# Hybrid attention and recurrence layer: K's norm buffers, the K/V weight splits and the recurrence's sums of squares put elsewhere

## The chip, the cores and the metric

The kernel runs on one core of a Trainium2 chip. The metric is the device time of one execution in microseconds (us); before and after are compared as medians of several runs. A trace of one execution, taken by the hardware profiler, is the other source: its times count from the start of its span. The engines are TensorE (PE: matrix products; its weight loads are PEld), VectorE (DVE), ScalarE (ACT), GpSimd (POOL) and SyncE (SP, which only starts transfers). Each works through its own instructions in a fixed order and waits on semaphores.

## The reference

One layer over 512 tokens with 2048 features, in float32. Cut to what matters:

```python
h = rms_norm(x, norm_w)
proj = einsum('bsd,de->bse', h, w_in)
q, k, v, g_attn, xr, g_lru = split(proj, SPLITS)
# attention: 8 query heads, 2 key/value heads of 128
q, k = rms_norm per head, then axial rotation
attn_out = softmax(q k^T / sqrt(128)) v
# recurrence: 8 blocks of 128 features, two directions
xc = conv_4_taps(xr) + conv_b
r = sigmoid(xc wa + ba);  i = sigmoid(xc wx + bx)
log_a = -8 * r * softplus(-lam);  a = exp(log_a)
h_t = a_t * h_(t-1) + sqrt(-expm1(2 log_a)) * (i * xc)     # forward and backward, summed
mixed = concat(rms_norm(attn_out) * silu(g_attn), rms_norm(lru_out) * silu(g_lru))
out = x + einsum('bse,ed->bsd', mixed, w_out)
```

## The kernel before, in words

**Products.** Every float32 matrix is split into a high half (a cast by ScalarE, line 228 for weights) and a low half (a subtraction by VectorE, line 229). A product of two such matrices is three products on TensorE: high-high, high-low and low-high (`mm3`, lines 153 to 155).

**Projections.** The weights of a projection come in chunks of 256 rows by 512 columns: `wload` starts a transfer of one chunk into a ring of three slots (`wring`, transfer on line 215) and splits it in two tiles (`wsplit`). The split tiles go into four buffers each for high and low in the pool `xw`; once the pool `wx` has been opened (inside `kv`), every second tile goes there, and there are eight. A projection of 512 columns takes eight chunks. For K/V and Q it is `proj_tok`, which calls `tok_block`: for each chunk c and each of four token tiles t it issues six products (one "unit", two row tiles of three products) into the PSUM bank of t, and yields. So a bank is complete in the last of the eight chunks, and the four banks of tag `pj` are evicted by ScalarE with a scale (`evac_tok`, line 629) before the next projection may write them.

**Stages and weaving.** The products of TensorE stand in the order in which they are written. `weave(fill, chain)` advances the projection by as many units as the chain of other work yields. In order: the recurrence's inputs (two halves of 512 columns), K and V together, Q's first half, Q's second half, the gates woven with attention, and the output. The recurrence's blocks are computed in pairs: the first four blocks (half 0) beside the second input projection, the last four (half 1) beside the K/V projection, and K's and V's own work (`kv`) beside Q's.

**Order on the other engines.** ScalarE, VectorE and, in these stages, SP and GpSimd are ordered when the program is built: a greedy scheduler gives each engine, whenever it is free by the scheduler's own timing, the ready instruction of highest priority. Priority is the place in the program; `tc.high_priority(n)` moves a block's place n instructions forward (AHEAD is 600 for weights, 300 for the recurrence's convolution; without n it goes to the front). `tc.issue_after(ins)`, and `behind(those)` for several, put the instructions of a block behind `ins` in the queue of its own engine. The order is then fixed, and on the chip each engine keeps to it.

**The recurrence** (`lru_pair`, two blocks at a time): split of the gates' weights and convolution (lines 532 to 548); after `steps[b]` units, twelve products per block and four sigmoids (line 559); the gating multiply i * xc (line 563); after `rest` units, tanh (569), exp (575) and sqrt (579) on ScalarE, then on VectorE the multiplies 582 and 583, two scans (586) and the sum of both directions (591). Its tiles lie in the pool `lru`, which is closed after the last pair. The pools `rot`, `qkv` and `wx`, opened later, get their places in memory that `lru` had, and their tiles wait for the release of the tiles that lay there.

**K and V** (`kv`, beside Q): K's norm and rotation (`norm_rope`: squares of each head with a sum on line 641, an inverse root by GpSimd on 374 and 375, multiplies on 646 to 655) in buffers of `rot`; at unit 20 the split of V (695, 696); then the recurrence's sums of squares (`lru_squares`, lines 596 to 603: four squares by ScalarE, the last three in one buffer `hsq`, each added by VectorE, and a last add by GpSimd); then K is turned (291), written to DRAM (299) and read back (321); at units 46 and 50 its two heads are split (685); then the sums are halved (854 to 857), and at unit 54 a product with ones (863) spreads them over all partitions. Its result is turned into an inverse root (864, 868), and the recurrence's outputs are multiplied with it (873). Q's first half passes through the same `norm_rope` and is turned and sent aside at unit 32, its second half after unit 64. Attention's first heads are split on line 685 as well.

**Sums of output weights.** Beside all this, SP copies rows of `w_out` in DRAM (936, behind the last weight transfer in SP's queue) and GpSimd starts adding transfers (939), from Q's first half on behind its own last inverse root.

Of the kernel before, what the change touches and what calls it, by code (L numbers as in the profile page):

```python
# [63 lines left out]
def hybrid_kernel(  # L64
# [373 lines left out]
    def tok_block(acc, w, r0, c0, lh, ll, nk):  # L438

        acc += [pj() for _ in range(NT)]  # L440
        for c in range(nk // 2):
            ws = wload(w, r0 + c * 2 * P, c0)
            for t in range(NT):
                ts_ = slice(t * P, (t + 1) * P)
                for k, (wh, wl) in enumerate(ws):
                    kk = 2 * c + k
                    mm3(acc[t], lh[kk][:, ts_], ll[kk][:, ts_], wh, wl, kk == 0, kk == nk - 1)
                yield c, t

    def proj_tok(c0, acc):  # L450
        yield from tok_block(acc, w_in, 0, c0, xh, xl, KT)
# [55 lines left out]
    def lru_half(half, acc, done=()):  # L507
# [13 lines left out]
        for b in range(0, 4, 2):  # L521
            bs = slice(b, b + 2)
            steps = ((6, 4, 8, 4), (10, 7, 9, 6))[half][bs]
            yield from lru_pair(4 * half + b, xrs[bs], grs[bs], steps, 99 if half and b else 0, mm if half else pj)

    def lru_pair(n0, xrs, grs, steps, rest, bank):

        xcs, cs, rs, is_, ths = [], [], [], [], []
        for n, xr, gr in zip((n0, n0 + 1), xrs, grs):
            with tc.high_priority(AHEAD // 2):  # L530
# [18 lines left out]
                cs.append((gh, gl, ch, cl))  # L549
        for b, n in enumerate((n0, n0 + 1)):  # L550
# [11 lines left out]
            i = is_[b]  # L562
            nc.vector.tensor_mul(i, i, xcs[b][:, None, :].broadcast_to([P, 2, SEQ]))
        yield rest
        for b, n in enumerate((n0, n0 + 1)):
            ths.append(b4())
            for d in range(2):
                j = d * NB + n
                nc.scalar.activation(
                    ths[b][:, d, :], rs[b][:, d, :], AF.Tanh, scale=c2[:, j : j + 1]  # L570
                )
# [21 lines left out]
    def lru_squares():  # L593

        hsum = pools["rot"].tile([P, 2, SEQ], F32, tag="hsum", name="hsum")
        nc.scalar.activation(hsum, hp[0], AF.Square)
        for pair in hp[1:]:
            yield 2
            sq = pools["rot"].tile([P, 2, SEQ], F32, tag="hsq", bufs=1, name=nm("hsq"))
            nc.scalar.activation(sq, pair, AF.Square)  # L600
# [32 lines left out]
    def norm_rope(es, nh, tab):  # L633
# [3 lines left out]
        for e in es:  # L637
            r = pools["rot"].tile([P, nh], F32, tag=f"rr{nh}", bufs=NT, name=nm("rr"))
            for h in range(nh):
                sq = pools["rot"].tile([P, HD], F32, tag="sh", bufs=1, name=nm("sh"))  # L640
# [3 lines left out]
        for t, (e, r) in enumerate(zip(es, rs)):  # L644
            sq = pools["rot"].tile([P, nh, HD], F32, tag="sq", bufs=2, name=nm("sq"))
# [41 lines left out]
    def kv(es):  # L687
        turned_k = sent(norm_rope(es, NKV, rk), NKV)
# [8 lines left out]
        yield from lru_squares()  # L697
# [4 lines left out]
        for h in range(NKV):  # L702
# [3 lines left out]
            those = split_head(pair, h, kth[h], ktl[h])  # L706
        parts = halved(
# [613 lines left out]
    def kv_proj():  # L1321
        yield from proj_tok(C_K, a3)
# [10 lines left out]
    def q_proj(c0, acc):  # L1333
        yield from proj_tok(c0, acc)
        rot[:] = norm_rope(evac_tok(acc, ev), G, rq)
# [181 lines left out]
```

## Time and profile before

| what | value |
|---|---|
| median of 3 runs | 627.7 us (627.63 to 629.04) |
| the profiled execution | 627.59 us |
| its span, first to last instruction | 625.8 us |
| TensorE busy in the span | 618.3 us |
| VectorE | 495.0 us |
| ScalarE | 359.7 us |
| GpSimd | 104.4 us |

Stages in the profiled execution, read off TensorE's order: K/V from about 106 to 161 us with four groups of gate products of half 1 among them, Q's first half from about 161, its second half from about 207, the gates and attention from about 251, the output stage from about 469.

How rows are read. In a row in order of time: start (us), time it took (us; of all of them together where xN stands at the end), engine, line, operation, what it writes `<-` what it reads, shapes; in brackets the idle time of the engine just before it and what ended that. In a group by line the two numbers behind the first bar are the busy time in us and the mean of one in ns, behind the second bar the idle time ahead. In the list of waits: who, for whom, us in total, times, the longest. A PE row lasts longer than the distance between two starts, because products overlap in the pipeline; the pace is the distance.

### The profile page before, as it was taken

Reading aid. Unit: us, or ns where it says so; the run is one execution under the profiler, and the core shown is the slowest. Engines: PE = TensorE matmul, PEld = TensorE weight load, DVE = VectorE, ACT = ScalarE, POOL = GpSimd, SP = SyncE. Lnnn points to the kernel's source line nnn. Section 1 sums busy time; section 2 is a strip of 40 time slices with the busy share of each in tenths; the row PEclk is TensorE's granted clock in tenths of the full one; section 3 lists DMA queues with packets and bytes.
Section 4 is the critical chain, followed back from the end, with each engine's and each line's share of the span. In section 5 each row is a group of like instructions: output and inputs, shape, how many; then the busy total and the mean of one; then the engine's idle time right before and its main releaser. Section 6 shows DMA issues by size and latency. Waiting matters only on the chain.

```text
span 625.8 us, 8286 instructions
## 1 busy us (share of the span) xinstructions
PE 618.3 (99%) x2740; PEld 510.2 (82%) x2740; DVE 495.0 (79%) x785; ACT 359.7 (57%) x646; POOL 104.4 (17%) x142
## 2 busy tenths in 40 slices
PE   9999999999999899999999999999999999999997
PEld 7888888887888688888888888888888888888886
DVE  6874878997798886887887887549979866886885
ACT  4596689959945833645485547338346633443441
POOL 3001111112003532622123222100210101011000
PEclk9999999999999999999999999999999999999999
DMA  8999958678674499579569646932995677797342
GB/s 292 309 330 276 209 140 207 149 186 197 181 229 152 152 209 248 128 199 272 171 197 261 201 136 185 261 92 77 282 251 190 211 254 246 264 362 217 135 135 101
DMA packets 75498, 129.71 MB, mean 207 GB/s; under 512 B 6872, under 2 KB 30528, under 8 KB 75456
## 3 DMA queue, kind: packets, MB, share of 16 engines
q1 hardware_dynamic: 67344, 111.70, 57.2%
q0 software_dynamic: 7936, 17.36, 14.7%
q8 instruction: 21, 0.34, 0.2%
q14 instruction: 21, 0.17, 0.1%
q10 hardware_dynamic: 176, 0.14, 0.1%
HBM read 111.34 MB, written 38.80 MB: 240 GB/s over the span
## 4 chain that ended last, share of the span: by engine, by line
PE 88%; ACT 5%; DVE 4%; issue 1%; DMA 1%; POOL 0%; ACTq 0%
PE pj L153 15%; PE pj L154 15%; PE pj L155 15%; PE mm L1067 14%; PE pj L1067 11%; PE mm L155 5%; PE mm L154 5%; PE mm L153 5%; PE pj L418 2%; ACT wh L228 1%; DVE wl L229 1%; DMA wr<-in_w_in_dram 1%; DVE b L586 1%; PE mm L263 1%; ACT b L559 1%
## 5 line engine op out<-in xcount | busy, mean ns | idle before, releaser
L228 ACT CAST wh<-wr 128x512 fp32r<-128x512 f32 x142 | 84.7, 618 | 85.9 <-PE pj L154 32.3
L154 PE MATMUL pj<-x,wh 128*128 128x512 f32 x304 | 118.3, 389 | 0.0
L155 PE MATMUL pj<-x,wl 128*128 128x512 f32 x304 | 118.3, 389 | 0.0
L153 PE MATMUL pj<-x,wh 128*128 128x512 f32 x304 | 118.3, 389 | 0.0
L229 DVE TENSOR_TENSOR wl<-wr,wh 128x512 fp32r<-128x512 f32 x144 | 98.9, 712 | 20.4 <-ACT wh L228 18.4
L915 ACT CAST wh<-wr 128x1024 fp32r<-128x1024 f32 (+1 forms) x72 | 60.6, 860 | 76.1 <-PE mm L1067 37.5
L916 DVE TENSOR_TENSOR wl<-wr,wh 128x1024 fp32r<-128x1024 f32 (+1 forms) x72 | 68.6, 983 | 30.1 <-ACT wh L915 30.0
L153 PE MATMUL pj<-wh,x 128*128 128x512 f32 x192 | 74.9, 390 | 2.3 <-ACT ev L629 2.3
L154 PE MATMUL pj<-wl,x 128*128 128x512 f32 x192 | 74.9, 390 | 0.2 <-DVE wl L229 0.2
L155 PE MATMUL pj<-wh,x 128*128 128x512 f32 x192 | 74.7, 389 | 0.0
L154 PEld LDWEIGHTS pj<-x,wh 128*128 128x128 f32 x304 | 57.1, 188 | 11.9
L153 PEld LDWEIGHTS pj<-x,wh 128*128 128x128 f32 x304 | 57.1, 188 | 11.9
L155 PEld LDWEIGHTS pj<-x,wl 128*128 128x128 f32 x304 | 57.1, 188 | 11.8
L939 POOL DMA_DIRECT2D t<-in_w_out_dram x40 | 33.3, 896 | 134.5 <-DMA t<-in_w_out_dram 77.6
L1067 PE MATMUL mm<-wh,ml 128*128 128x512 f32 x126 | 49.0, 389 | 0.0
L1067 PE MATMUL mm<-wh,mh 128*128 128x512 f32 x126 | 49.0, 389 | 0.0
L1067 PE MATMUL mm<-wl,mh 128*128 128x512 f32 x126 | 49.0, 389 | 0.0
L153 PEld LDWEIGHTS pj<-wh,x 128*128 128x128 f32 x192 | 36.0, 188 | 10.3 <-ACT ev L629 2.9
L154 PEld LDWEIGHTS pj<-wl,x 128*128 128x128 f32 x192 | 36.0, 188 | 8.0 <-DVE wl L229 0.6
L155 PEld LDWEIGHTS pj<-wh,x 128*128 128x128 f32 x192 | 36.0, 188 | 7.5
L739 POOL TENSOR_SCALAR p<-p,sm 128x512 f32<-128x512 f32 x32 | 23.6, 742 | 89.7 <-DVE sm L738 89.7
L1067 PE MATMUL pj<-wl,mh 128*128 128x512 f32 (+1 forms) x100 | 38.5, 385 | 0.0
(229 smaller groups left out, 1167.7 us busy)
## 6 DMA issues: line engine op xcount, KB each, us to landing
wr<-in_w_in_dram SPq DMA_DIRECT2D x71, 512.0 KB, 5.1
wr<-in_w_out_dram SPq DMA_DIRECT2D x21, 512.0 KB, 5.2
t<-in_w_out_dram POOLq DMA_DIRECT2D x40, 256.0 KB, 7.5
wr<-t SPq DMA_DIRECT2D x40, 256.0 KB, 5.3
pd<-u SPq DMA_DIRECT2D x16, 512.0 KB, 3.5
pt<-pd SPq DMA_DIRECT2D x64, 128.0 KB, 4.0
t<-in_w_out_dram SPq DMA_DIRECT2D x24, 256.0 KB, 5.2
wr<-in_w_out_dram SPq DMA_DIRECT2D x22, 256.0 KB, 4.9
```

Source lines behind the costliest of these rows:

```text
L153: nc.tensor.matmul(acc, lh, rh, start=start, stop=False)
L154: nc.tensor.matmul(acc, lh, rl, start=False, stop=False)
L155: nc.tensor.matmul(acc, ll, rh, start=False, stop=stop)
L228: copy(hi, raw[:, k, :]).ins,
L229: nc.vector.tensor_sub(lo, raw[:, k, :], f(hi)).ins,
L263: nc.tensor.transpose(pt[:, t * P : (t + 1) * P], xc[:, t, ks], ident)
L418: nc.tensor.matmul(acc[e], w[:, e * P : (e + 1) * P], x_[2 * c + k], start=c == k == j == 0, stop=False,)
L739: last_pool[0] = nc.gpsimd.tensor_scalar(p, p, sm, 0.0, op0=ALU.mult, op1=ALU.add).ins
L915: nc.scalar.copy(hi[:, to], b)
L916: nc.vector.tensor_sub(lo[:, to], b, f(hi[:, to]))
L939: nc.gpsimd.dma_start(dst, src, accum_op=ALU.add)
L1067: nc.tensor.matmul(dst[s][:, es], lh[:, ts_], rh[:, es], start=i == ends_[0] and j == 0, stop=i == ends_[1] and j == 2,)
```

## The change

- `tok_block` gets `early`: with 1, a chunk's transfer and split are written one chunk ahead of its products. The K/V projection uses it.
- In half 1, the first pair's `rest` is 4 units instead of 0, and the second pair's first step 5 instead of 9, so that the gate products keep their places. In that pair the tanh instructions are queued behind the last weight cast written by then (chunk 6 of K/V), and the gating multiplies move behind the tanh in the program and behind that chunk's splits in their queue.
- `norm_rope` is told its pool. K's buffers go to `rope`, which is open since the start, under tags of their own; Q's stay in `rot`.
- `lru_squares` moves from V's split to four units behind K's second head, with its squares behind that head's cast in ScalarE's queue (its other member, VectorE's subtraction, binds nothing here, as only the squares stand in that block). The steps of `kv` are then: V at unit 20, K turned and sent at 22, read back at 28, heads at 40 and 44, squares from 48, halving at 54, the product with ones at 58.

```diff
@@ -435,11 +435,14 @@
                     mm3(acc[e], wh[:, es], wl[:, es], xh[kk], xl[kk], kk == 0, kk == KT - 1)
                 yield c, e
 
-    def tok_block(acc, w, r0, c0, lh, ll, nk):
+    def tok_block(acc, w, r0, c0, lh, ll, nk, early=0):
 
         acc += [pj() for _ in range(NT)]
+        ahead = []
         for c in range(nk // 2):
-            ws = wload(w, r0 + c * 2 * P, c0)
+            for n in range(c + len(ahead), min(c + 1 + early, nk // 2)):
+                ahead.append(wload(w, r0 + n * 2 * P, c0))
+            ws = ahead.pop(0)
             for t in range(NT):
                 ts_ = slice(t * P, (t + 1) * P)
                 for k, (wh, wl) in enumerate(ws):
@@ -447,8 +450,8 @@
                     mm3(acc[t], lh[kk][:, ts_], ll[kk][:, ts_], wh, wl, kk == 0, kk == nk - 1)
                 yield c, t
 
-    def proj_tok(c0, acc):
-        yield from tok_block(acc, w_in, 0, c0, xh, xl, KT)
+    def proj_tok(c0, acc, early=0):
+        yield from tok_block(acc, w_in, 0, c0, xh, xl, KT, early)
 
     def weave(fill, chain):
 
@@ -520,8 +523,8 @@
             xrs = [*done, *evac_bc(acc[len(done) :])]
         for b in range(0, 4, 2):
             bs = slice(b, b + 2)
-            steps = ((6, 4, 8, 4), (10, 7, 9, 6))[half][bs]
-            yield from lru_pair(4 * half + b, xrs[bs], grs[bs], steps, 99 if half and b else 0, mm if half else pj)
+            steps = ((6, 4, 8, 4), (10, 7, 5, 6))[half][bs]
+            yield from lru_pair(4 * half + b, xrs[bs], grs[bs], steps, (4, 99)[b // 2] if half else 0, mm if half else pj)
 
     def lru_pair(n0, xrs, grs, steps, rest, bank):
 
@@ -547,6 +550,12 @@
                 nc.scalar.copy(ch, xc)
                 nc.vector.tensor_sub(cl, xc, f(ch))
                 cs.append((gh, gl, ch, cl))
+
+        def gated(b):
+            nc.vector.tensor_mul(
+                is_[b], is_[b], xcs[b][:, None, :].broadcast_to([P, 2, SEQ])
+            )
+
         for b, n in enumerate((n0, n0 + 1)):
             yield steps[b]
             gh, gl, ch, cl = cs[b]
@@ -559,16 +568,21 @@
                     nc.scalar.activation(
                         dst[:, d, :], pg, AF.Sigmoid, bias=v1(bias + d * NB + n)
                     )
-            i = is_[b]
-            nc.vector.tensor_mul(i, i, xcs[b][:, None, :].broadcast_to([P, 2, SEQ]))
+            if not 0 < rest < 99:
+                gated(b)
         yield rest
         for b, n in enumerate((n0, n0 + 1)):
             ths.append(b4())
             for d in range(2):
                 j = d * NB + n
-                nc.scalar.activation(
-                    ths[b][:, d, :], rs[b][:, d, :], AF.Tanh, scale=c2[:, j : j + 1]
-                )
+                with behind(split_done[-1][:1] if 0 < rest < 99 else ()):
+                    nc.scalar.activation(
+                        ths[b][:, d, :], rs[b][:, d, :], AF.Tanh, scale=c2[:, j : j + 1]
+                    )
+        if 0 < rest < 99:
+            for b in range(2):
+                with behind(split_done[-1]):
+                    gated(b)
         for b, n in enumerate((n0, n0 + 1)):
             for d in range(2):
                 j, r = d * NB + n, rs[b][:, d, :]
@@ -590,14 +604,16 @@
                 hp[n // 2] = hring.tile([P, 2, SEQ], F32, name=nm("hs"))
             nc.vector.tensor_add(hp[n // 2][:, b, :], i[:, 0, :], i[:, 1, :])
 
-    def lru_squares():
+    def lru_squares(those):
 
         hsum = pools["rot"].tile([P, 2, SEQ], F32, tag="hsum", name="hsum")
-        nc.scalar.activation(hsum, hp[0], AF.Square)
+        with behind(those):
+            nc.scalar.activation(hsum, hp[0], AF.Square)
         for pair in hp[1:]:
             yield 2
             sq = pools["rot"].tile([P, 2, SEQ], F32, tag="hsq", bufs=1, name=nm("hsq"))
-            nc.scalar.activation(sq, pair, AF.Square)
+            with behind(those):
+                nc.scalar.activation(sq, pair, AF.Square)
             nc.vector.tensor_add(hsum, hsum, sq)
         sums["l"] = hsum[:, 0, :]
         nc.gpsimd.tensor_add(sums["l"], sums["l"], hsum[:, 1, :])
@@ -630,19 +646,19 @@
                 res.append(e)
         return res
 
-    def norm_rope(es, nh, tab):
+    def norm_rope(es, nh, tab, home, n=""):
 
         es = [e[:, : nh * HD].rearrange("p (h d) -> p h d", d=HD) for e in es]
         rs = []
         for e in es:
-            r = pools["rot"].tile([P, nh], F32, tag=f"rr{nh}", bufs=NT, name=nm("rr"))
+            r = pools[home].tile([P, nh], F32, tag=f"rr{n}", bufs=NT, name=nm("rr"))
             for h in range(nh):
-                sq = pools["rot"].tile([P, HD], F32, tag="sh", bufs=1, name=nm("sh"))
+                sq = pools[home].tile([P, HD], F32, tag=f"sh{n}", bufs=1, name=nm("sh"))
                 nc.scalar.activation(sq, e[:, h, :], AF.Square, accum_out=r[:, h : h + 1])
             rsqrt_mean(r, r, HD, nh)
             rs.append(r)
         for t, (e, r) in enumerate(zip(es, rs)):
-            sq = pools["rot"].tile([P, nh, HD], F32, tag="sq", bufs=2, name=nm("sq"))
+            sq = pools[home].tile([P, nh, HD], F32, tag=f"sq{n}", bufs=2, name=nm("sq"))
             nc.vector.tensor_mul(e, e, r[:, :, None].broadcast_to([P, nh, HD]))
             for s in range(2):
                 nc.vector.tensor_mul(
@@ -685,7 +701,7 @@
         return nc.scalar.copy(hi, src).ins, nc.vector.tensor_sub(lo, src, f(hi)).ins
 
     def kv(es):
-        turned_k = sent(norm_rope(es, NKV, rk), NKV)
+        turned_k = sent(norm_rope(es, NKV, rk, "rope", "k"), NKV)
         yield 20
         opened("wx", "right")
         for t in range(NT):
@@ -694,7 +710,6 @@
             vh[t], vl[t] = vt[:, 0, :], vt[:, 1, :]
             nc.scalar.copy(vh[t], vv)
             nc.vector.tensor_sub(vl[t], vv, f(vh[t]))
-        yield from lru_squares()
         yield 2
         drain(turned_k)
         yield 6
@@ -704,6 +719,8 @@
             kt = pools["qkv"].tile([P, 2, SEQ], F32R, tag="kt", bufs=NKV, name=nm("kt"))
             kth[h], ktl[h] = kt[:, 0, :], kt[:, 1, :]
             those = split_head(pair, h, kth[h], ktl[h])
+        yield 4
+        yield from lru_squares(those)
         parts = halved(
             sums["l"],
             lambda: pools["rope"].tile([P, SEQ], F32R, tag="kv", bufs=NT, name=nm("kv")),
@@ -1319,7 +1336,7 @@
     kvs = []
 
     def kv_proj():
-        yield from proj_tok(C_K, a3)
+        yield from proj_tok(C_K, a3, 1)
         kvs.extend(
             evac_tok(
                 a3, lambda: pools["rope"].tile([P, SEQ], F32, tag="kv", bufs=NT, name=nm("kv"))
@@ -1332,7 +1349,7 @@
     opened("qkv", "right")
     def q_proj(c0, acc):
         yield from proj_tok(c0, acc)
-        rot[:] = norm_rope(evac_tok(acc, ev), G, rq)
+        rot[:] = norm_rope(evac_tok(acc, ev), G, rq, "rot")
 
     def both():
         yield from q_proj(C_Q, a4)
```

## The prediction

> **What bounds the kernel now.** I read the page's busy shares first, then PE's waits, then PE, ScalarE and VectorE in order of time around each wait.
>
> ```profile
> PE 618.3 (99%) x2740; PEld 510.2 (82%) x2740; DVE 495.0 (79%) x785; ACT 359.7 (57%) x646; POOL 104.4 (17%) x142
> PE pj L153 <- ACT ev L629: 2.3, 1, 2.3
> PE pj L154 <- DVE wl L229: 0.2, 1, 0.2
> PEld mm L155 <- DVE q L685: 0.3, 1, 0.3
> 204.49 0.39 PE L155 MATMUL pj<-wh,x 128*128 128x512 f32 x1
> 207.13 0.50 PE L153 MATMUL pj<-wh,x 128*128 128x512 f32 x1 [2.26 <-ACT ev L629]
> 207.47 0.40 PE L154 MATMUL pj<-wl,x 128*128 128x512 f32 x1
> 214.00 0.39 PE L155 MATMUL pj<-wh,x 128*128 128x512 f32 x1
> 144.43 0.39 PE L153 MATMUL pj<-wh,x 128*128 128x512 f32 x1
> 144.98 0.50 PE L154 MATMUL pj<-wl,x 128*128 128x512 f32 x1 [0.16 <-DVE wl L229]
> 145.32 0.39 PE L155 MATMUL pj<-wh,x 128*128 128x512 f32 x1
> 188.39 0.39 PE L153 MATMUL pj<-wh,x 128*128 128x512 f32 x1
> 189.30 0.39 PE L154 MATMUL pj<-wl,x 128*128 128x512 f32 x1
> ```
>
> TensorE is busy 99% of the span, so only its gaps can be won. In a stretch without gaps four products start 189.30 - 188.39 = 0.91 us apart: 0.227 us each, 1.36 us a unit of six, 5.44 us a chunk of 24. Against that pace the two gaps ahead of the places that the change touches cost:
>
> - K/V chunk 6: from 144.43 to 145.32 two steps take 0.89 us where 0.45 would do: **0.44 us**. The low half of the weights came late.
> - Q's second half: from 204.49 to 207.47 two steps take 2.98 us: **2.53 us** lost. The next 28 steps, to 214.00, take 6.53 us for 6.35: **0.18 us** more.
>
> All that can be won is 0.44 + 2.53 + 0.18 = 3.15 us, 0.5% of 627.59 us. A measurement of this kernel can tell about 0.3%, which is 1.9 us, so the large gap alone decides between faster and the same.
>
> Why the large gap is there:
>
> ```profile
> 202.54 1.06 ACT L600 ACTIVATE hsq<-hs 128x1024 f32<-128x1024 f32 x1 [4.34 <-DVE hsum L601]
> 204.93 1.06 ACT L600 ACTIVATE hsq<-hs 128x1024 f32<-128x1024 f32 x1 [0.81 <-DVE hsum L601]
> 206.40 0.68 ACT L629 ACTIVATE ev<-pj,rstd 128x512 f32<-128x512 f32 x1
> 201.23 1.22 DVE L601 TENSOR_TENSOR hsum<-hsum,hsq 128x1024 f32<-128x1024 f32 x1
> 186.29 3.09 DVE L229 TENSOR_TENSOR wl<-wr,wh 128x512 fp32r<-128x512 f32 x5
> ```
>
> The second half of Q needs the PSUM banks of the first. The first half's last chunk starts 5.44 us ahead of the second half's due time, 204.49 + 0.23 = 204.72, so at 199.28, and the first bank gets its last product one unit later, near 200.6. Its eviction (L629) runs at 206.40, nearly 6 us later. ScalarE stood 4.34 us in front of a sum of squares, which has one buffer and waits for VectorE's add of the one before, and VectorE reached that add (201.23) only between K's rotations. The evictions were queued behind it.
>
> **The change, part by part.** No operation is added or removed on any engine; buffers and the order change.
>
> *Squares behind K's heads.* Four squares, three adds, GpSimd's add and the halving leave the stretch before 206. The first bank can then be evicted near 201.3 (200.6 plus 0.68) and is wanted at 204.7. Each later bank is ready and wanted one unit after the one before, so the spare time of some 3.4 us holds for all four. Are the second half's weights next in line? Q chunk 5 starts three chunks ahead of 204.72, at 188.39, and at 189.38 VectorE had split five tiles from there on, two and a half chunks: they are not. Gain 2.53 + 0.18 us.
>
> What the move costs: the all-ones product (L863) that spreads the sums stands in TensorE's written order, and goes from unit 54 to unit 58 of Q.
>
> ```profile
> 237.34 0.40 PE L863 MATMUL mm<-kv,ones_r 128*128 128x512 f32 x1
> 207.39 1.60 POOL L603 TENSOR_TENSOR hsum<-hsum 128x512 f32<-128x512 f32 x1 [8.81 <-DVE hsum L601]
> 227.86 1.24 DVE L685 TENSOR_TENSOR kt<-lq,kt 128x512 fp32r<-128x512 f32 x2
> 229.12 0.69 DVE L857 TENSOR_TENSOR kv<-hsum,kv 64x512 fp32r<-64x512 f32 x1
> 225.43 0.81 POOL L939 DMA_DIRECT2D t<-in_w_out_dram  x1 [3.77 <-issue]
> ```
>
> It comes at 237.34 + 5.44 - 3.15 = 239.63. Its operand was ready at 229.81 (the end of L857), with 7.5 us to spare. Now the chain starts late. At worst nothing of it runs before K's heads are through VectorE, at 229.10 - 3.15 = 225.95 (Q's rotation holds VectorE until then). From there: three adds (3.7) with two squares between them (2.1), GpSimd's 1.60, and the three steps of the halving at 0.69 (2.1; the first two put at the row of the third): 9.5 us. With 0.2 us at each of seven hand-overs (an estimate; from the add's end at 202.45 to the square at 202.54 it was 0.09) and four weight splits of 0.62 let in ahead: 13.4 us, ready at 239.4. GpSimd's add (L603) also moves past the DMA adds that GpSimd issues from 219 on; where one of them stands before it, as the one that waited 3.77 us to issue, the end is 243.2. At the other end the adds have slipped into VectorE's gaps before Q's rotation, and only GpSimd's step and the halving follow: 4.5 us, ready at 230.4. Needed is 239.63. I take zero: the DMA adds leave GpSimd free most of the time, and VectorE's gaps take the first adds. For the range: 0 to 3.6 us.
>
> The spread being later, its followers are later too:
>
> ```profile
> 246.54 1.22 DVE L873 TENSOR_TENSOR hs<-hs,gbc 128x1024 f32<-128x1024 f32 x1
> 251.67 0.69 DVE L646 TENSOR_TENSOR ev<-ev,rr 128x512 f32<-128x512 f32 x1 [3.91 <-POOL rr L375]
> 265.86 1.28 DVE L685 TENSOR_TENSOR q<-lq,q 128x512 fp32r<-128x512 f32 x2
> ```
>
> From the product at 237.34 to the last of the four normalizing multiplies at 247.76 VectorE's train takes 10.4 us, then idles 3.91 us. From 239.63 it would end at 250.05, while the rotation of Q's second half wants VectorE at 251.67 - 3.15 = 248.52. That overlap is 1.5 us. The rotation leads to the split of attention's first query (265.86), for which TensorE already waits a little (the 0.3 us row). So 0 to 1.5 us comes back there. The rotation goes first by its place in the program, so it waits for less than one multiply: I take **0.5 us**.
>
> *K's buffers with the rotation tables.* K's squares no longer wait for memory that the recurrence holds, as they did until 187.77:
>
> ```profile
> 185.69 2.19 ACT L228 CAST wh<-wr 128x512 fp32r<-128x512 f32 x4 [2.59 <-DVE b L586]
> 187.77 0.31 ACT L641 ACTIVATE sh<-kv 128x128 f32<-128x128 f32 x1
> 182.47 0.62 ACT L228 CAST wh<-wr 128x512 fp32r<-128x512 f32 x1 [4.13 <-PE pj L155]
> 219.29 1.14 ACT L685 CAST kt<-lq 128x512 fp32r<-128x512 f32 x2 [2.02 <-DMA lq<-qd]
> ```
>
> ScalarE waits of 4.13 and 2.59 us stand before 182.47 and 185.69; the eight squares, 0.31 us each with a short readout behind, fit in there. VectorE's part follows the recurrence's scans, so K is turned and sent aside several us earlier, and its heads land before 219. On SP the write and four reads back pass in front of weight loads; those run chunks ahead of TensorE, so they hide it. Worth nothing by itself: no wait of TensorE is for K.
>
> The danger is the other way. A K multiply let in between two dependent steps of the recurrence delays the last scan (L586), on which the cast at 185.69 waits for its memory. That cast belongs to Q chunk 5, whose low halves are the first two of the five at 186.29, done near 187.5; TensorE wants the second at 189.30, or 188.86 once it is 0.44 us ahead. About 1.3 us to spare, against one multiply of some 0.4 us: zero, up to 0.3 us if ScalarE's part of the recurrence also slips by two casts.
>
> *Weights ahead of the tangents.*
>
> ```profile
> 140.25 1.95 ACT L569 ACTIVATE b<-b,c 128x512 f32<-128x512 f32 x3
> 142.09 1.14 ACT L228 CAST wh<-wr 128x512 fp32r<-128x512 f32 x2
> 143.12 1.21 DVE L563 TENSOR_TENSOR b<-b,k 128x1024 f32<-128x1024 f32 x1
> 144.25 1.28 DVE L229 TENSOR_TENSOR wl<-wr,wh 128x512 fp32r<-128x512 f32 x2
> 154.58 2.35 DVE L583 TENSOR_TENSOR b<-b,b 128x1024 f32<-128x1024 f32 x2
> ```
>
> Chunk 6's casts (142.09) stand behind three tangents, and its low halves (144.25) behind a gating multiply. The casts' buffers come free with chunk 4's last products, 5.44 us before 144.43, at 139. Put first, the casts end near 141.5 and the low halves near 142.5, two us in time: the 0.44 us goes. The last tangent still ends when it did, since the same instructions fill the same time; the gating multiplies come some 2.5 us later, and are first read at 154.58. The second pair's convolution is written four units (5.44 us) later, but VectorE takes it by readiness, long before its own products. The earlier loads change nothing, as a load waits for its ring slot; the copies of the output weights that SP holds behind the last load come up to a chunk later and are first read in the output stage.
>
> **Sum.** 0.44 + 2.53 + 0.18 - 0.5 = 2.65 us. The profiled execution took 627.59 us (span 625.8), 0.11 below the median of the runs: 624.94 against it, so **625.0 us** for the median.
>
> **Rivals.**
>
> *Eaten* (0.13): ScalarE and VectorE take K's work in front of the recurrence's in several places, and the last scan is 3 us late. Then chunk 5 waits 3 - 1.3 = 1.7 us: 626.7 us. For it: the recurrence and K meet on both engines, and both orders are the scheduler's. Against: the recurrence's steps stand earlier in the program.
>
> *Not what it says* (0.06): another blocked instruction stands before the evictions, K's head cast waiting for its transfer, as it did 2.02 us at 219.29. K is now ready earlier, so this wait comes nearer to 201 to 205. It must exceed the 3.4 us to spare. If it restores the gap, only 0.44 us is left: 627.1 us.
>
> *Spread late by one wait* (0.08): the chain's worst end, behind one DMA add: TensorE waits 243.2 - 239.63 = 3.6 us at L863, 628.6 us.
>
> *Slower* (0.14): the squares chain stands behind waits of both engines. With one DMA add before GpSimd's step (3.77) and one square on ScalarE behind a cast that waits for TensorE (the 4.13 us row), the operand comes at 239.4 + 7.9 = 247.3; TensorE waits 7.7 us at L863: 632.7 us. It is slower by over 0.3% from a wait of 2.65 + 1.9 = 4.5 us, an operand after 244.1. For it: the chain has little to spare at its worst end, and before, both kinds of wait fell into this stretch. Against: it needs VectorE to have no gap for the adds from 205 on, too.
>
> *GpSimd in the recurrence's way* (0.03): K's inverse roots would run beside the last scans.
>
> ```profile
> L375 POOL TENSOR_TENSOR rr<-rr,nhalf 128x2 f32<-128x2 f32 x4 | 3.2, 810 | 0.3
> L374 POOL TENSOR_SCALAR rr<-rr 128x2 f32<-128x2 f32 x4 | 1.8, 456 | 44.9 <-ACT sh L641 44.9
> 190.89 0.75 POOL L375 TENSOR_TENSOR rr<-rr,nhalf 128x2 f32<-128x2 f32 x1
> 190.68 0.42 DVE L696 TENSOR_TENSOR v<-kv,v 128x256 fp32r<-128x256 f32 x1
> 191.75 0.42 DVE L654 TENSOR_TENSOR kv<-kv,rk 128x256 f32<-128x256 f32 x1
> ```
>
> If each held VectorE for its whole time, the last scan would be 3.2 + 1.8 = 5.0 us late and chunk 5 would wait 3.7 us: 628.7 us, within 0.3%. Against: a two-input VectorE operation that ran into GpSimd's power at 190.89 took 0.42 us, as the one without it at 191.75. [...]
>
> **How the numbers follow.** My forecast has 0.56. It reaches from 624.4 (nothing given back), less some scatter, to 625.8 (the 0.3% bound). Eaten, not what it says, the spread late by one wait and GpSimd's hold lie within 0.3%: 0.13 + 0.06 + 0.08 + 0.03 = 0.30. Slower: 0.14. The range runs from 624.0, since runs of one kernel scatter (627.63 to 629.04 before), to 628.6, which takes in all that lies within 0.3% but GpSimd's hold, and leaves out the slower one.
>
> **What would show it.** Right: no wait of TensorE for L629 and none for L229 near 144; the eviction at 201 to 203 with no L600 before it; L641 on K before 182; L600 and L601 after K's L685; L863 without a gap near 239.6, its operand's last step (L857) before that. Wrong: a gap at L863, one at Q's chunk 5 near 188, or over 1 us at attention's first product near 263.

## The result, and the profile after

| | before | after |
|---|---|---|
| median of 4 runs each, on one chip | 628.37 us (627.63 to 629.39) | 638.43 us (636.71 to 638.56) |
| ratio, 95% interval | | 1.0153 [1.0128, 1.0178] |
| the profiled execution; its span | 627.59 us; 625.8 us | 638.56 us; 636.8 us |

The kernel after is slower by 1.5%, where 625.0 us was forecast. Its line numbers are shifted; the first column below is the line of the kernel before.

| before | after | what it is |
|---|---|---|
| L559, L569 | L568, L579 | sigmoid, tanh of the recurrence |
| L601, L603 | L617, L619 | VectorE's add of squares, GpSimd's last add |
| L629, L641 | L645, L657 | eviction, square of a head |
| L685 | L701 | split of a head |
| L854, L857, L863 | L871, L874, L880 | first and last step of the halving, spread product |
| L939 | L956 | adding transfer that GpSimd starts |

First the page's line of busy times and all waits of TensorE that the view of waits lists (us in total, times, longest).

```profile
PE 622.7 (98%) x2740; PEld 512.7 (81%) x2740; DVE 494.7 (78%) x785; ACT 359.9 (57%) x646; POOL 107.2 (17%) x142
PE mm L880 <- DVE kv L874: 6.6, 1, 6.6
PE pj L154 <- DVE wl L229: 1.4, 1, 1.4
PE mm L155 <- DVE q L701: 0.9, 1, 0.9
PE mm L1213 <- PEq L1519: 0.8, 1, 0.8
PE mm L153 <- ACT b L568: 0.4, 2, 0.2
```

The eviction's wait of before (2.3 us) is gone, as forecast: the first bank is evicted when TensorE is through with it.

```profile
203.78 0.69 ACT L645 ACTIVATE ev<-pj,rstd 128x512 f32<-128x512 f32 x1 [0.74 <-PE pj L155]
```

In the wait's place stand the spread product's, one at Q chunk 5, one at attention's first query, and two short ones of the last gate products for the sigmoids. VectorE and ScalarE are as busy as before. Now the largest, TensorE in order of time:

```profile
242.79 0.39 PE L155 MATMUL pj<-wh,x 128*128 128x512 f32 x1
249.79 0.80 PE L880 MATMUL mm<-kv,ones_r 128*128 128x512 f32 x1 [6.61 <-DVE kv L874]
250.38 0.63 PE L153 MATMUL pj<-wh,x 128*128 128x512 f32 x1
250.81 0.63 PE L154 MATMUL pj<-wl,x 128*128 128x512 f32 x1
```

Between two starts lie 7.00 us where 0.23 would do: 6.77 us lost. Behind it the pace is wrong as well, 250.81 - 250.38 = 0.43 us for 0.227. The view by stretches (the fraction before the DMA share is the granted clock) shows why:

```profile
230.00:242.00 12.00, 12.00 (x55) 9.94 (x54) 4.01 (x5) 2.42 (x4) 3.27 (x4) 1.00 1.07 280
242.00:250.00 8.00, 1.39 (x7) 0.85 (x6) 1.61 (x3) 1.60 (x3) 2.95 (x3) 0.73 1.12 244
250.00:256.00 6.00, 6.00 (x15) 4.70 (x16) 4.52 (x7) 1.36 (x3) 0.00 (x0) 0.51 0.35 97
256.00:262.00 6.00, 6.00 (x28) 4.97 (x27) 3.45 (x4) 4.60 (x17) 1.23 (x2) 1.00 0.01 3
```

TensorE worked at half clock (0.51) until 256: 15 products in 6 us, against 28 in the next 6. From 249.79 to the first start at full pace (256.16) that costs another 2.96 us. Together the place costs 9.73 us.

What it waited for, first VectorE's part of the chain, then GpSimd's queue:

```profile
232.71 1.23 DVE L617 TENSOR_TENSOR hsum<-hsum,hsq 128x1024 f32<-128x1024 f32 x1 [1.13 <-ACT hsq L616]
...
247.68 0.69 DVE L871 TENSOR_TENSOR hsum<-hsum 64x512 f32<-64x512 f32 x1 [12.54 <-POOL hsum L619]
```

```profile
221.74 2.58 POOL L956 DMA_DIRECT2D t<-in_w_out_dram  x3
227.72 0.81 POOL L956 DMA_DIRECT2D t<-in_w_out_dram  x1 [3.39 <-issue]
...
235.49 0.81 POOL L956 DMA_DIRECT2D t<-in_w_out_dram  x1 [4.08 <-issue]
...
245.53 0.82 POOL L956 DMA_DIRECT2D t<-in_w_out_dram  x1 [0.75 <-issue]
246.09 1.56 POOL L619 TENSOR_TENSOR hsum<-hsum 128x512 f32<-128x512 f32 x1
```

The three adds on VectorE are done at 233.94. GpSimd's add, 1.56 us of work, starts 12.15 us later: eleven adding transfers stand before it in GpSimd's queue (the three of the first row and eight single ones), and they go out with pauses of up to 4.08 us. In the kernel before the add stood in front of all of them, at 207.39.

The smaller places, TensorE in order of time at the gates' last products, Q chunk 5 and attention's first query:

```profile
160.40 0.50 PE L153 MATMUL mm<-k,k 128*128 128x512 f32 x1 [0.19 <-ACT b L568]
...
161.56 0.50 PE L153 MATMUL mm<-k,k 128*128 128x512 f32 x1 [0.19 <-ACT b L568]
...
189.57 0.44 PE L153 MATMUL pj<-wh,x 128*128 128x512 f32 x1
191.45 0.51 PE L154 MATMUL pj<-wl,x 128*128 128x512 f32 x1 [1.44 <-DVE wl L229]
...
276.34 0.39 PE L154 MATMUL mm<-kt,q 128*128 128x512 f32 x1
277.63 0.50 PE L155 MATMUL mm<-kt,q 128*128 128x512 f32 x1 [0.90 <-DVE q L701]
```

Two of the last gate products' groups start 1.16 us apart where three products at 0.227 take 0.68; with 0.11 us behind them, 1.07 us. Chunk 5 loses 1.88 - 0.23 = 1.65 us at the pair and some 0.1 behind it; attention 1.29 - 0.23 = 1.06.

The budget from span to span: -0.44 (K/V chunk 6) - 2.71 (evictions) + 1.07 (gates) + 1.7 (chunk 5) + 9.73 (spread) + 1.07 (attention) + 0.4 (lost in the first 20 us, which the change does not touch) = 10.8 of 11.0 us.

### The profile page after: what moved, and what is told of

Same layout as the page of the kernel before. It is cut to its first block, busy times and chain, and to the rows that moved or that the text cites. A ratio compares the mean times of both kernels' runs of the same rounds, so it can differ in the third digit from the quotient of the medians.

```text
span 636.8 us, 8279 instructions
## 1 busy us (share of the span) xinstructions
PE 622.7 (98%) x2740; PEld 512.7 (81%) x2740; DVE 494.7 (78%) x785; ACT 359.9 (57%) x646; POOL 107.2 (17%) x142
## 4 chain that ended last, share of the span: by engine, by line
PE 86%; ACT 4%; issue 4%; DVE 3%; POOL 2%; DVEq 0%; POOLq 0%
PE pj L154 15%; PE pj L153 15%; PE pj L155 15%; PE mm L1084 13%; PE pj L1084 10%; PE mm L155 5%; PE mm L153 5%; PE mm L154 5%; PE pj L418 2%; POOL t L956 1%; DVE wl L229 1%; ACT sh L657 1%; ACT wh L228 1%; DVE b L600 1%; PE mm L1213 1%
## 5 line engine op out<-in xcount | busy, mean ns | idle before, releaser
L153 PE MATMUL pj<-wh,x 128*128 128x512 f32 x192 | 75.9, 395 | 0.0
L155 PE MATMUL pj<-wh,x 128*128 128x512 f32 x192 | 75.7, 394 | 0.0
L956 POOL DMA_DIRECT2D t<-in_w_out_dram x40 | 33.3, 892 | 131.7 <-DMA t<-in_w_out_dram 76.6
L153 PEld LDWEIGHTS pj<-wh,x 128*128 128x128 f32 x192 | 36.8, 192 | 7.8 <-ACT wh L228 0.2
L155 PEld LDWEIGHTS pj<-wh,x 128*128 128x128 f32 x192 | 36.6, 191 | 7.7
```

The source lines that it names most:

```text
L153: nc.tensor.matmul(acc, lh, rh, start=start, stop=False)
L155: nc.tensor.matmul(acc, ll, rh, start=False, stop=stop)
L956: nc.gpsimd.dma_start(dst, src, accum_op=ALU.add)
```

## The experiments

The patch has three separable parts: the weights (early loads, tanh and gating behind the splits), K's buffers, and the move of the squares. Times in us, with the ratio to the kernel before on the same chip.

| run | edit | median | ratio, 95% interval |
|---|---|---|---|
| e_vadd | after, last add on VectorE | 628.67 | 1.0005 [0.9994, 1.0015] |
| e_weights | before + weights | 629.67 | 1.0026 [1.0014, 1.0037] |
| e_kbufs | before + K's buffers | 627.51 | 0.9993 [0.9980, 1.0006] |
| e_squares | before + squares moved | 632.81 | 1.0075 [1.0055, 1.0094] |
| e_sq_vadd | the former, last add on VectorE | 626.31 | 0.9976 [0.9967, 0.9985] |
| e_latesums | after, adding transfers kept out of Q's stage | 633.91 | 1.0111 [1.0088, 1.0134] |
| e_clock | after, 50 small products before the spread | 636.95 | 1.0145 [1.0118, 1.0172] |
| e_clock80 | after, 80 of them | 637.62 | 1.0143 [1.0128, 1.0157] |
| e_kb_hold | before + K's buffers, K's norm held back | 626.02 | 0.9975 [0.9965, 0.9984] |
| e_lite | before + a gentler weights' part | 628.96 | 0.9999 [0.9986, 1.0012] |
| e_hold_prio | e_kb_hold, squares more urgent | 625.67 | 0.9954 [0.9942, 0.9967] |
| e_hold_prio_lite | the former + e_lite | 625.63 | 0.9954 [0.9941, 0.9967] |

The theory after the result ("queue"): the large loss is GpSimd's add behind the adding transfers. Its rival ("chain"): the moved squares are too late by themselves, on ScalarE and VectorE.

**e_vadd**, the whole change with one operation on another engine:

```diff
-        nc.gpsimd.tensor_add(sums["l"], sums["l"], hsum[:, 1, :])
+        nc.vector.tensor_add(sums["l"], sums["l"], hsum[:, 1, :])
```

> The changed kernel, with the last add of the squares (hsum's two halves) on VectorE instead of GpSimd. Theory 'queue': the spread product was late because this add stood behind eleven DMA adds in GpSimd's queue; VectorE had finished its third add at 233.94 us, nine us before the product was due at 243.0. On VectorE the wait of 6.8 us goes, and with it the 3.0 us of the stretch at half clock behind it: 638.4 - 9.8 = 628.6 us. Rival 'chain': the squares themselves come too late behind Q's rotation, whoever adds last; then a wait of at least 3 us stays at the product and the time stays above 632 us.

The chain on VectorE, and TensorE's spread product in the place where 6.6 us were lost:

```profile
232.48 1.23 DVE L617 TENSOR_TENSOR hsum<-hsum,hsq 128x1024 f32<-128x1024 f32 x1 [1.13 <-ACT hsq L616]
...
234.82 0.69 DVE L619 TENSOR_TENSOR hsum<-hsum 128x512 f32<-128x512 f32 x1
...
236.92 0.69 DVE L874 TENSOR_TENSOR kv<-hsum,kv 64x512 fp32r<-64x512 f32 x1 [0.69 <-ACT kv L873]
...
243.04 0.40 PE L880 MATMUL mm<-kv,ones_r 128*128 128x512 f32 x1
```

The third add of the squares is as late as in the kernel after (232.48 against 232.71), and the operand is still ready 5.4 us early. No wait, no half clock (the granted clock of the execution is 1.000): "chain" falls, and the 9.7 us belong to the place in the queue. The three smaller gaps remain, so this version only comes back to the time of before.

**e_weights, e_kbufs, e_squares**: each part alone, cut out of the change's diff (shown there). K's buffers, for example, are this line with the tags that go with it:

```diff
-        turned_k = sent(norm_rope(es, NKV, rk), NKV)
+        turned_k = sent(norm_rope(es, NKV, rk, "rope", "k"), NKV)
```

> The kernel before with the weights' part alone (early splits in K/V, the first pair's tangents and gating multiplies behind chunk 6's splits). Theory 'tangents': pushing the tangents back delays the recurrence on ScalarE by 2 us or more, so the new gaps at the last group of gate products (1.0 us) and at Q's chunk 5 (1.7 us) belong to this part: chunk 6's 0.44 us is gained, 1 to 2.5 us lost, 628.3 to 630 us. Rival 'K ahead': those gaps come from K's buffers alone; then this part is 0.4 us faster than before, about 627.6 us, with no new gap.

The theory about the tangents held. Chunk 6's gap goes, and the gates' gap appears, with the same two waits. ScalarE in the kernel after shows how:

```profile
140.79 1.14 ACT L228 CAST wh<-wr 128x512 fp32r<-128x512 f32 x2
144.25 0.62 ACT L550 CAST k<-k 128x512 fp32r<-128x512 f32 x1 [2.32 <-DVE k L545]
144.78 2.56 ACT L579 ACTIVATE b<-b,c 128x512 f32<-128x512 f32 x4
```

The casts are early, but with the tanh ordered behind them ScalarE then stands 2.32 us in front of a cast that waits for the second pair's convolution on VectorE; the tanh, which filled that time before, end at 147.34 instead of 143.85. All behind them, the last sigmoids too, comes later. The evictions' gap of 2.31 us stays, as it should.

> The kernel before with K's norm buffers moved alone. Theory 'tangents': at most one K operation gets between the recurrence's steps, and Q's chunk 5 waits 0 to 0.5 us; the time is that of before within 0.5 us, and the wait for the evictions at 207 us stays or shrinks a little. Rival 'K ahead': the gaps at the gate products (1.0 us) and at chunk 5 (1.7 us) are here: 629 to 631 us.

This was a surprise both ways. The evictions' gap is gone without the squares being moved, and a gap at chunk 5 takes its place (e_kbufs in order of time, ScalarE, VectorE and TensorE):

```profile
163.29 2.42 ACT L559 ACTIVATE b<-mm,vec 128x512 f32<-128x512 f32 x4
...
185.26 0.42 DVE L646 TENSOR_TENSOR kv<-kv,rr 128x256 f32<-128x256 f32 x1
185.59 2.33 DVE L586 TENSOR_TENSOR_SCAN b<-b,b 128x512 f32<-128x512 f32 x2
...
190.78 0.50 PE L154 MATMUL pj<-wl,x 128*128 128x512 f32 x1 [1.65 <-DVE wl L229]
...
201.20 1.06 ACT L600 ACTIVATE hsq<-hs 128x1024 f32<-128x1024 f32 x1 [0.29 <-DVE hsum L601]
...
203.19 0.68 ACT L629 ACTIVATE ev<-pj,rstd 128x512 f32<-128x512 f32 x1
```

K's rotation goes through VectorE earlier, so the adds of the recurrence's squares come earlier too, and the last square no longer stands before the evictions (201.20; before, at 204.93). But five of K's squares now run on ScalarE ahead of the last four sigmoids (163.29; 161.17 before), and a K multiply slips in between the last multiply and the last scans. The last scan ends at 187.92 instead of 185.65, and chunk 5, whose casts wait for its memory, loses 1.9 us. The two nearly cancel: the time is that of before.

> The kernel before with the squares moved alone. Theory 'queue': 2.7 us are gained at the evictions, and the spread product waits 6 to 9 us with a stretch at half clock of 3 us behind it: 628 - 2.7 + 10 to 12 = 635 to 637.5 us. Rival 'chain': the wait needs the other two parts as well (K's work turned round in VectorE's queue); then it is under 2 us here, and the time 625 to 627 us.

The measured wait lies between the two expectations: 3.38 us, with 13 products at half pace behind it (0.43 us from start to start), where "queue" had 6 to 9 us and "chain" less than 2. GpSimd in e_squares:

```profile
212.88 2.59 POOL L942 DMA_DIRECT2D t<-in_w_out_dram  x3
...
238.93 0.82 POOL L942 DMA_DIRECT2D t<-in_w_out_dram  x1 [1.11 <-issue]
239.49 1.55 POOL L605 TENSOR_TENSOR hsum<-hsum 128x512 f32<-128x512 f32 x1
```

The mechanism is the same, add behind the same eleven transfers, 11 us after VectorE's last (228.48). But the transfers end 6.6 us earlier here than in the kernel after, and the spread is due only 3.4 us earlier, without that kernel's other delays. The expectation had taken the transfers' time from the kernel after. The traces show where the difference arises: the transfers stand behind GpSimd's last inverse root for Q's first half, which ends at 212.92 here and at 221.78 there, so they start 8.9 us earlier and then take 2.3 us longer.

**e_sq_vadd** has both edits, squares moved and the add on VectorE, without the other two parts.

```diff
-        yield from lru_squares()
...
+        yield 4
+        yield from lru_squares(those)
...
+        nc.vector.tensor_add(sums["l"], sums["l"], hsum[:, 1, :])
```

> The kernel before with the squares moved and their last add on VectorE, without the other two parts. Theory: the eviction's 2.7 us are won, the spread product is in time, and only attention's first query comes 1.1 us later, since the normalizing multiplies now lie before Q's second rotation: 628.0 - 2.7 + 1.1 = 626.4 us. Rival: with the heads later than in the changed kernel, the product waits 1 us or more: 627.5 us or above.

As expected: 2.4 per thousand faster than before. Besides chunk 6's short wait, the one for attention's first query remains (1.0 us). Every version with the squares moved has a wait of 0.9 to 1.0 us there and none of the others has, so it comes with the move; that the later normalizing multiplies cause it is argued, not tested.

**e_latesums** leaves the add on GpSimd and moves the transfers instead.

```diff
-    fill = with_sums(both(), 3)
+    fill = with_sums(both(), 3, 0, 31)
```

> The changed kernel with the DMA adds of the output weights kept out of Q's stage (they start with the gates); the add of the squares stays on GpSimd. Theory 'queue': what was wrong is the place behind eleven DMA adds, not the engine: the spread product doesn't wait, 628.7 us as with the add on VectorE. Rival: GpSimd's add is late for another reason (its input, its own time of 1.6 us); then a wait of some us stays, 632 to 638 us. Either could lose a few us more in attention, where GpSimd then has more to do.

The spread product no longer waits, which confirms "queue" from the other side: the add is still on GpSimd and starts at 233.69, right behind its operand. But the time is 633.91 and not the 628.7 of the theory. From 302 to 336 us, in attention, the profiled execution falls 4.4 us behind that of e_vadd, and TensorE's list of waits gets new entries there, where GpSimd's share of that work now stands between the transfers (that the one causes the other was not tested):

```profile
PE mm L153 <- ACT ph L776: 2.0, 1, 2.0
...
PE mm L154 <- DVE pl L776: 1.3, 2, 0.8
```

**e_clock and e_clock80** ask whether the slow pace behind the wait is a price of TensorE's standing still. Small products on constants, whose result nobody reads, fill the wait.

```diff
+        w2 = mm()
+        for _ in range(80):
+            nc.tensor.matmul(w2[:, : 2 * P], wv[:, :P], wv, start=True, stop=True)
         spread(gbc, parts, NB * P)
```

> The changed kernel with 50 small products on constants (256 columns, written to a bank of their own and read by nobody) in TensorE's order just ahead of the spread product, in the 7 us in which it waits. Theory 'clock': the 14 products at 0.43 us behind the wait (3.0 us) ran at half clock because TensorE had stood still, as the granted clock of 0.51 in that stretch says; busy, it keeps the clock, the spread product still starts near 249.8 us, and 3 us go: 635.4 us. Rival 'transfers': the slow products come from transfers or late weights; they stay slow and the time stays at 638 us.

> The kernel after with 80 small products (bfloat16, 256 columns, on constants, into a bank that is free; 0.116 us each in the run with 50) put before the spread product, so that TensorE is busy for 9.3 us where it waited 6.6: they cover the whole wait. Theory 'clock' (the half-pace stretch behind the wait comes from TensorE having stood idle before it): no product at 0.427 us behind the spread product, the granted clock near 1.00 in the windows behind it, in every run; the stretch cost about 3.0 us and the products outlast the wait by some 2.5 us, so the time is about 638.4 - 3.0 + 2.5 = 637.9, and the trace, not the time, tells. Rival (the slow stretch belongs to what else runs there, such as the DMA adds or the operands' arrival): the 13 products at 0.427 us stand behind the spread product all the same, and the time is 640.5 or more.

With 50 a wait of 2.72 us remained in the profiled execution, and three products later the pace halved again: the clock was 0.57 from 252 to 256. Two of the four runs, the profiled one among them, had a granted clock of 0.997 (638.30 and 638.87 us); the other two kept the clock (0.999 and 1.000) and took 634.38 and 635.61 us, near the 635.4 of theory "clock". With 80 the wait is covered (TensorE in order of time, and the clock by stretches, of e_clock80):

```profile
242.96 9.15 PE L732 MATMUL mm<-const-bfloat16-1.0 128*128 128x256 bf16 x80
251.86 0.48 PE L883 MATMUL mm<-kv,ones_r 128*128 128x512 f32 x1
```

```profile
252.00:256.00 4.00, 4.00 (x19) 3.29 (x19) 2.90 (x4) 1.31 (x2) 0.00 (x0) 1.00 0.34 117
```

Full clock, although the same transfers run and the same operand arrives. All four runs had a granted clock of 0.999 or 1.000, against 0.990 to 0.995 in the kernel after. So the half pace follows TensorE's idleness here: 0.51 behind 6.61 us of it, 1.00 behind none.

**e_kb_hold** keeps K's buffers and queues K's norm behind the recurrence's last square root and last scan, so that it cannot push in.

```diff
+                tail[:1] = [nc.scalar.activation(t, t, AF.Sqrt, scale=-1.0).ins]
...
+        with behind(tail):
+            turned_k = sent(norm_rope(es, NKV, rk, "rope", "k"), NKV)
```

> The kernel before with K's norm buffers moved, and K's norm queued behind the recurrence's last square root on ScalarE and its last scan on VectorE. With the buffers alone the wait for the evictions was gone, and Q's chunk 5 waited 1.9 us, since five of K's squares stood before the last sigmoids (2.1 us) and one multiply between two steps of the recurrence. Theory 'K ahead': held back, K leaves the recurrence alone; the eviction's wait stays away as K still ends earlier than before. 628.0 - 2.7 = 625.3 us. Rival: the evictions were only in time because K's squares went first; held back, the sums of squares block ScalarE again and the time is 627 to 628 us.

Chunk 5's gap is gone, so K's pushing in was its cause. The evictions wait 0.44 us again, so the time lies between the 625.3 of the theory and the 627 of its rival.

**e_lite** keeps the early loads and the gating multiplies behind chunk 6's splits, but leaves tanh and exponentials where they were.

```diff
+            for b in range(2):
+                with behind(split_done[-1]):
+                    gated(b)
```

> The kernel before with the weights' part made gentler: K's loads one chunk early, and the gating multiplies of half 1's first pair moved behind the splits of chunk 6, but its tangents, exponentials and the rest where they were. Theory 'tangents' (the gates' gap of 1.05 us in the kernel with the whole weights' part comes from the tangents, which wait there for VectorE's split and push the last sigmoids later on ScalarE): no gap at the gate products, the 0.44 us at chunk 6 gone, so the time is about 0.4 us below that of the kernel before (ratio 0.9993). Rival (the gap comes from the moved multiplies or the loads): a gap of about 1.0 us stays at the gate products, and the time is 0.6 us or more above that of the kernel before (ratio 1.001 or more).

The trace agrees with the tangents' theory: TensorE has no gap at chunk 6 and none at the gates. The time does not show the 0.44 us: the evictions' wait of this run is 3.1 us instead of 2.3, eight of its eleven runs have a granted clock of 0.997, and by the interval nothing is proved either way.

**e_hold_prio** adds urgency to the recurrence's squares in e_kb_hold, and **e_hold_prio_lite** adds e_lite's edit to that.

```diff
+            with tc.high_priority(AHEAD):
+                nc.scalar.activation(sq, pair, AF.Square)
+                nc.vector.tensor_add(hsum, hsum, sq)
```

> The kernel with K's norm buffers moved and K's norm held behind the recurrence's last square root and last scan (626.0 us against 627.6), with the squares of the recurrence and their adds made more urgent in ScalarE's and VectorE's order. Theory (what is left of the gap at Q's evictions, 0.44 us of wait and 0.3 us of start-up, comes from ScalarE standing 5.2 us in front of a square that waits for VectorE's add): the gap goes, and the time is about 0.7 us lower, ratio to the kernel before 0.9964. Rival (ScalarE is late there for the mass of its work): the gap stays or moves, ratio 0.9975 as before.

> The former with the gentler weights' part. If both theories hold, the terms add: chunk 6's 0.44 us besides, ratio to the kernel before about 0.9957, some 625.0 us. If the gates' gap comes back, 626.3 or more.

ScalarE of e_hold_prio at the first eviction, and TensorE's wait for weights in its list of waits (0.18 at K/V chunk 6, 0.48 at Q chunk 5):

```profile
195.63 1.06 ACT L605 ACTIVATE hsq<-hs 128x1024 f32<-128x1024 f32 x1
...
201.85 0.69 ACT L634 ACTIVATE ev<-pj,rstd 128x512 f32<-128x512 f32 x1 [0.74 <-PE pj L155]
```

```profile
PE pj L154 <- DVE wl L229: 0.7, 2, 0.5
```

The last square is done five us before the eviction, which now waits for TensorE, as it should. This version is 0.46% under the kernel before, and only the next one is as fast. A part of that is the clock of the kernel before: ten of its fifteen runs in this comparison have a granted clock of 0.997, and against the median of the other five (627.41 us) the gain is 1.7 us, as between the two traces. The gentler weights' part on top of it adds nothing that can be measured: chunk 6's gap goes and chunk 5's grows a little (0.57 us of wait for 0.48). The terms did not add.

## Why the prediction was wrong

The gains came as forecast: 0.44 us at chunk 6, and 2.71 us at the evictions for 2.53 + 0.18. Every loss was put too low.

- **The step that failed: "I take zero: the DMA adds leave GpSimd free most of the time".** That GpSimd is idle 83% of the span doesn't help an instruction that stands behind eleven others in its queue. The prediction named the queue and then let one of them (3.77 us) stand before the add. The code has one transfer in three units, from Q's first half's last inverse root on, so about eight of them are written before the add at unit 54; the queue of the kernel after has all eleven ahead of it. The trace of before had the same eleven, from 219.08 on, and the last of them went out 15 us after the spread's operand was ready there (229.81):

```profile
244.72 0.82 POOL L939 DMA_DIRECT2D t<-in_w_out_dram  x1 [2.98 <-issue]
```

In the kernel after the add started 12.15 us after its operand, and the spread lost 6.77 us.
- **The half pace was no term at all.** 2.96 us came on top, from a fall of the clock to 0.51 that the wide gap (2.26 us) in the trace of before had not shown: there the clock stayed at 1.00 from 206 to 220, and the next 28 steps lost only 0.18 us. e_clock80 ties the fall to the idleness.
- **The chain on ScalarE and VectorE was sized well**, though VectorE's gaps did not take the first adds, as the prediction hoped: the first one came at 228.05, behind K's heads. The prediction gave the chain 4.5 to 13.4 us from the end of K's heads; with the add on GpSimd and no transfer ahead of it, it took 10.9 us (227.11 to 238.00 in e_latesums), in time for the spread at 242.89. The spread itself was due 3.4 us later than the prediction's 239.63, by the losses ahead of it.
- **"The last tangent still ends when it did" was wrong**, by 3.5 us. It counted instructions and not what the engine waits for: in the old order the tanh filled a wait for VectorE's convolution, and in the new order nothing does. Price 1.07 us at the gates (also in e_weights; gone in e_lite).
- **K's buffers "worth nothing by itself" was wrong in both directions.** They alone remove the evictions' gap, and they alone cost 1.9 us at chunk 5 (e_kbufs). The prediction saw the K multiply between the recurrence's steps, but not K's squares ahead of the sigmoids on ScalarE. It had given that course to the rival *Eaten*, with the last scan 3 us late and a price of 1.7 us. In the kernel after the scan is 3.15 us late (188.80 for 185.65) and chunk 5 loses 1.7 us. That the price fits is partly chance: TensorE was itself 1.2 us late there, and the spare time was less than the 1.3 us taken, as TensorE goes on when the third of the five low halves ends (191.40), not the first or second.
- **Attention's first query**: 1.07 us, within the 0 to 1.5 given, twice the 0.5 taken.
- **The rivals.** *Slower* had the place and the sign, and its wait of 7.7 us is close to 6.77. The closeness is luck, for its mechanism was another: one transfer, and a square behind ScalarE's casts; the runs show eleven transfers, and only 1.13 us of wait for the last square. Its total of 632.7 us lacked the half pace and the smaller losses. *Spread late by one wait* had the place too, with one transfer and 3.6 us. *GpSimd in the recurrence's way* did not happen in the direction it named (below). *Not what it says* did not happen.

## What to carry to other kernels

When an instruction moves past others on an engine with little to do, count what stands before it in that queue and when the last of it can go; the share of busy time says nothing of it. Price a wait of TensorE above its own length: here 6.61 us of it were followed by 6 us at a clock of 0.51, which cost another 2.96 us. And an edit that only frees buffers changes the order too: ask which instructions become ready early, and what they then push in front of.

## What the runs showed of the hardware

**The clock after a gap.** The gap of 6.6 us was followed by half pace (clock 0.51 from 250 to 256), and one of 3.38 us as well (e_squares, 13 products 0.43 us apart). Shorter ones did it in part of the executions: 3.09 us in e_lite's trace (clock 0.57 from 207 to 211, five products at half pace), 2.72 us in e_clock's (0.57 from 252 to 256) and 2.31 us in e_weights' (0.59 from 209 to 213), but 2.26 us in the trace of before did not (1.00 from 206 to 220).

```profile
208.87 0.50 PE L153 MATMUL pj<-wh,x 128*128 128x512 f32 x1 [2.31 <-ACT ev L642]
...
210.03 0.63 PE L154 MATMUL pj<-wl,x 128*128 128x512 f32 x1
210.46 0.63 PE L155 MATMUL pj<-wh,x 128*128 128x512 f32 x1
```

In e_weights the pace falls only 1.2 us after the work has resumed. The kernel before shows the same as two groups of times: of its 67 runs beside the experiments, 39 had a granted clock of 0.999 or 1.000 and a median of 627.41 us, and 28 had 0.997 and 629.24 us. So four runs in ten take 1.8 us more, which the prediction had taken for scatter. That the evictions' gap is the cause is inferred, as no such run of before was traced: of e_vadd, e_sq_vadd, e_kb_hold and e_hold_prio, where that gap is gone or 0.44 us long, none of 39 runs has the lower clock. But three of e_kbufs' twelve runs have 0.996, where the longest of these gaps in the traced execution is the 1.65 us at chunk 5; none of the three was traced. What decides whether a gap of 2 to 3 us is followed by half pace was not shown.

**GpSimd beside VectorE.** With K's inverse roots running beside the recurrence, GpSimd's power of two columns took 1.53 to 3.74 us in e_kbufs, for 0.75 to 0.96 us before; its first two:

```profile
160.48 1.56 POOL L375 TENSOR_TENSOR rr<-rr,nhalf 128x2 f32<-128x2 f32 x1
...
163.32 3.74 POOL L375 TENSOR_TENSOR rr<-rr,nhalf 128x2 f32<-128x2 f32 x1
```

VectorE's scans beside them kept their length (2.33 us for two, at 159.20 and at 180.09, as before). So GpSimd lengthens and VectorE doesn't; the cause was not tested.

**Left open**: why GpSimd's adding transfers go out with pauses of up to 4.08 us, and why the scheduler put the last three ahead of the add. The DMA engines were full in that stretch (a share of 1.07 from 230 to 242), which would fit the pauses, but no run varied it.
